# A hybrid attention block on one core: the order of all steps and the engine choices written out as lists, and small sums, casts and prefixes rewritten

## Chip, core and metric

The kernel runs on one NeuronCore of a Trainium2 chip. The metric is the device time of one execution in microseconds. Five engines work side by side, each through its own queue in program order: PE (TensorE, matmuls; PEld is its weight load), DVE (VectorE), ACT (ScalarE), POOL (GpSimd) and SP (SyncE, which here issues the DMAs). They wait for each other by semaphores only.

## What is computed

One block over 512 tokens of width 1024, all in float32, cut to the core:

```python
h = _rmsnorm(x, norm_g)
p_fox, p_ssm, p_nsa, p_mem = _split(h @ w_in, [...])
mem_kv = _rmsnorm(mem, mem_norm_g) @ w_mem_kv
o = concatenate([fox(p_fox), ssd(p_ssm), nsa(p_nsa), mem(p_mem, mem_kv)])
x = x + o @ w_out
return _rmsnorm(x, final_norm_g)
```

- fox: causal attention, 8 heads of 64, with a cumulative sum over the log of a forget gate added to the scores.
- ssd: a short convolution, then a chunked state space model (4 chunks of 128), and a norm over groups.
- nsa: for each block of 128 queries three softmaxes (over compressed blocks, selected blocks, a window), each with its own sigmoid gate, and their sum. With 512 tokens all eight blocks are selected.
- mem: attention of 4 heads of 128 over 256 memory tokens.

Each result is multiplied by silu of a gate; the four are projected by `w_out`.

## The kernel before

**Precision and tiles.** A float32 matrix is split into a rounded part and the remainder (`hi`, `lo`), and a product is three matmuls (`three`). The weights come in 75 tiles of 128 x 1024, one DMA each (`raw`), are rounded on ACT (`wh`), and the remainder is taken on POOL or DVE (`wl`, in `split`). A projection tile of 128 columns (`tile_a`) is 24 matmuls of 512 columns into one PSUM bank (`pj`), and a sink then reads the bank and makes the operands of a mixer. The output projection (`out_proj`, and `out_last` for the last mixer) writes `po` and adds it to `acc`. In the trace names without their numbers stand for tiles: `pS`, `pW` scores, `pN`, `pF`, `pM` softmax rows of nsa, fox and mem, `rs` the reciprocals of their sums, `pcp` nsa's compressed rows and `pT` their transposes, `fl`, `far`, `pt` the other rows on their way through a transpose in DRAM, `pO` the mixers' output, `pd` the prefix sums of the forget gates, `prm` the broadcast of the memory norm.

**The order.** The source runs once, in Python, and emits instructions. Everything goes through `Engine`, whose calls are noted in `Clock`, a model of all engines' times, buffers and DMAs. The projections stand in `ORDER` as background work (`Sched.todo`): one step emits three matmuls. The mixers are pipelines (`Pipe`) of stages: prep (p), ssm (s), fox (f), cmp (c), nsa (n), mem (m). In nsa, stage 0 is scores and softmax, stage 1 transposes, 2 and 3 the way to DRAM and back, 4 the product with the values and 5 the gate. `Sched.run` chooses a stage whose inputs are due by the modelled PE time, or else fills with a background step. Where an operation could run on two engines (`evac`, `rows_by`, `tt`), the engine that the model has free is taken. Buffers come from shared pools (`g` with 58 of 2 KB a partition, `b4` with 12, eight PSUM banks).

**What the change touches.** `smalls` makes gates, time steps and the forget gates' logs; `fox_bias` makes their cumulative sums: four prefix matmuls with a triangle `U`, and for blocks 1 to 3 a matmul with `ones` that adds all earlier blocks (`before`). `prep_mem` broadcasts the memory norm over all partitions by two matmuls into `prm`. In nsa's stage 0 the reciprocal of a softmax sum is made by three operations on DVE: a maximum with 1e-30, a reciprocal, a product with the gate. At the end `finish` squares a piece of a row block of the result, multiplies it by the norm's weights, and `end` makes the root and scales.

Of the kernel before, what the change touches and what calls it, by code (L numbers as in the profile page):

```python
# [32 lines left out]
LAST = 3  # L33
# [7 lines left out]
NARROW, AFTER, SLACK = 0, 500, 1000  # L41
PRE = 750

# [16 lines left out]
)  # L60
KEYS_A = [k for k in ORDER if k[0] not in ("bv", "bc", "mv") and k[0][:2] != "wo"]


class Clock:
# [4 lines left out]
    def __init__(self):  # L69
        self.t = dict.fromkeys(("PE", "ACT", "DVE", "POOL", "SP"), 700.0)  # L70
        self.dma = 0.0
        self.used = {}
        self.born = {}
        self.port = []
        self.tiled = False
        self.last = self.landed = self.sure = 0.0
        self.lanes = [0.0] * 8
        self.banks = []

# [11 lines left out]
    @staticmethod  # L91
    def box(x):

        if str(x.space).endswith("DRAM"):
# [11 lines left out]
    def at(self, x, eng=None, reading=True):  # L106
        t, u = self.born.get(x.name, 0.0), self.used.get(x.name)
        if u:
            a, b, c, d = self.box(x)
            bank = reading and str(x.space).endswith("PSUM")  # L110
            for ((e, f, g, h), by, wrote), end in u.items():
                end += self.HOP + (self.SPARE if eng == "PE" and by != "DMA" else 0)
                if by != eng and end > t and (
                        (wrote or not reading) and e < b and a < f and g < d and c < h or bank and not wrote):
                    t = end
# [5 lines left out]
    def slot(self, start, took):  # L121
# [7 lines left out]
        self.port.append((start, start + took))  # L129
        return start  # L130

    def note(self, eng, op, a, k):
# [5 lines left out]
        for x in ins:  # L138
            start = max(start, self.at(x, eng))
        for x in outs:  # L140
            if not str(x.space).endswith("DRAM"):
                start = max(start, self.at(x, eng, False))
# [3 lines left out]
        if eng == "PE":  # L146
# [8 lines left out]
            if start > self.t[eng] + 1700:  # L155
                took += 3300
        elif op == "dma_start":
            took = 430
            start = max(start, self.lanes.pop(0))
        elif eng == "ACT":  # L160
            near = str(wide[0].space).endswith("SB") if wide else True
# [8 lines left out]
        else:  # L170
            near = [x for x in wide if str(x.space).endswith("SB")]
# [8 lines left out]
            port = fast or len(near) > 1 and all(x.ap[-1][0] == 1 for x in (out, *ins))  # L180
            if any(self.box(x)[0] != self.box(out)[0] for x in wide):
# [8 lines left out]
        if op == "dma_start":  # L190
# [4 lines left out]
            both = str(out.space).endswith("DRAM") and str(ins[0].space).endswith("DRAM")  # L195
            away = str(out.space).endswith("DRAM")
# [8 lines left out]
        for xs, wrote in ((ins, False), (outs, True)):  # L205
            for x in xs:
                u = self.used.setdefault(x.name, {})
                b = self.box(x)
# [41 lines left out]

class Engine:
    def __init__(self, real, name, clock):
        self.real, self.name, self.clock = real, name, clock

    def __getattr__(self, op):
        f = getattr(self.real, op)

        def call(*a, **k):
            self.clock.note(self.name, op, a, k)
            return f(*a, **k)  # L260
# [3 lines left out]
class Sched:  # L264
    def __init__(self, clock, ready, ahead, soon, room):
        self.clock, self.ready, self.ahead, self.soon, self.room = clock, ready, ahead, soon, room
        self.todo, self.pipes = [], []
        self.done = set()

# [23 lines left out]
    def step(self):  # L293
        item = self.todo[0]
        for key, *_ in self.todo[:3]:
# [21 lines left out]

    def run(self, pipes):
        self.pipes = pipes = list(pipes)
        while pipes:  # L320
# [3 lines left out]
            now, best = self.now, None  # L324
            active = pipes[:ACTIVE]
            for pipe in active:
# [9 lines left out]
            if best[0] > now:  # L336
                t = self.due()
                if t <= now or t <= best[0]:
                    if t == math.inf:
                        raise RuntimeError(f"nothing can run: {self.todo[0][0]}, {[p.at for p in pipes]}")  # L340
                    self.fill()
# [3 lines left out]
            best[1].run(self, best[2])  # L345


class Pipe:
# [3 lines left out]
    def __init__(self, steps, stages, depth, banks, takes, keep, pre=None):  # L352
# [25 lines left out]
    def run(self, bg, k):  # L378
        i = self.at[k]
        bg.clock.last = 0.0  # L380
# [9 lines left out]
def block_kernel(ctx, tc, I, out):  # L390
    nc = tc.nc
    clock = Clock()
    V, A, P, T, Q = (Engine(e, n, clock) for e, n in (
# [3 lines left out]
    ps = ctx.enter_context(tc.tile_pool(name="ps", bufs=8, space=bass.MemoryType.PSUM))  # L397
# [3 lines left out]
    gs, bs = Store(NG), Store(NB)  # L401

    def G(name, dt=FT, w=512, p=128):
        gs.take()
        return sb.tile([p, w], dt, name=name, tag="g", bufs=NG)

    def B4(name, shape, dt=FT):
        bs.take()
        return sb.tile(shape, dt, name=name, tag="b4", bufs=NB)
# [4 lines left out]
    def SM(name, w):  # L414
        return sb.tile([128, w], FT, name=name, tag="sm", bufs=11)

    def MD(name, w):
        return sb.tile([128, w], FT, name=name, tag="md", bufs=7)

    def PS(name):  # L420
        t = ps.tile([128, 512], FT, name=name, tag="ps", bufs=8)
# [123 lines left out]

    def tt(bias, out, in0, in1, op):
# [4 lines left out]
        (V if onv + bias < onp else P).tensor_tensor(out=out, in0=in0, in1=in1, op=op)  # L551
# [134 lines left out]
    def ready(key):  # L686
        g, b = TAKES[key[0]]
        if key[0] in ("mv", "mk") and not mh:
            g, b = g + 4, b + 2
# [23 lines left out]
    def soon(key):  # L713
        if key[0] in ("mv", "mk") and (len(mh) or bg.room(4 + bg.kept(), 2)):
# [66 lines left out]
    def split_k(p, col, scale):  # L781
# [3 lines left out]
        for a in range(2):  # L785
# [3 lines left out]
            V.tensor_scalar(out=col(kx[0][a][y]), in0=p(x), scalar1=scale, scalar2=None, op0=OP.mult)  # L789
# [5 lines left out]
    def s_fq(p, key):  # L795
# [3 lines left out]
        for a in range(2):  # L799
# [3 lines left out]
            A.activation(M[a][y], ind[y, h:h + 1].to_broadcast([64, 512]), AF.Copy)  # L803
        R[key] = (R[key], M)

    def s_fk(p, key):
        l2 = B4("Rl", [128, 1024], FR)
        Rs, lo = [G("Rk", FR) for _ in range(2)], [l2[:, 512 * a:512 * a + 512] for a in range(2)]
        for a in range(2):
            x, y = slice(64 * a, 64 * a + 64), slice(64 - 64 * a, 128 - 64 * a)  # L810
            A.activation(Rs[a][x], p[x], AF.Copy)
            V.tensor_copy(out=lo[a][y], in_=cr()[y].bitcast(FT))
        for a in range(2):
            x, y = slice(64 * a, 64 * a + 64), slice(64 - 64 * a, 128 - 64 * a)
            V.tensor_copy(out=Rs[a][y], in_=p[x])
# [11 lines left out]
    def split_o(mixer):  # L827
        for j in range(4):
            if (mixer, j) in o_f and (mixer, j) not in o_hl:
                hi, lo = G("oh", FR), G("ol", FR)  # L830
                A.copy(out=hi, in_=o_f[mixer, j])
                tt(SOON, out=lo, in0=o_f[mixer, j], in1=hi.bitcast(FT), op=OP.subtract)
# [12 lines left out]
    def finish(t, i, c0, w, last):  # L845
# [15 lines left out]
        if t == 3:  # L861
            c_ = slice(384 * i, min(384 * i + 384, D))
            (V if i == 2 else P).tensor_tensor(out=fin["o"][:, c_], in0=a[:, c_], in1=g[:, c_], op=OP.mult)
        elif i == 0:
            P.tensor_tensor(out=a[:, cs], in0=a[:, cs], in1=g[:, cs], op=OP.mult)
        if last:
            fin["end"] = t, i, fs

    def end():
# [4 lines left out]
        v, r = SM("fw", 1), SM("fr", 1)  # L874
        V.tensor_reduce(out=v, in_=fs[:, 0:i + 2], axis=mybir.AxisListType.X, op=OP.add)
        P.tensor_tensor(out=r, in0=v, in1=nhalf[:, :1], op=OP.pow)
        if t == 3:
            o = fin["o"]
# [4 lines left out]
            return  # L883
        V.scalar_tensor_tensor(out=a[:, 512:1024], in0=a[:, 512:1024], scalar=r, in1=g[:, 512:1024],
# [40 lines left out]
    def out_last(t):  # L925
# [26 lines left out]
        "wo1": lambda k: out_last(k[1]) if LAST == 1 else out_proj(1, k[1]),  # L952
# [8 lines left out]
    crs, before = [], []  # L961

    def smalls():
# [20 lines left out]
        s4 = s4f.rearrange("p (t c) -> p t c", t=4)  # L984
        before.append(s4[:, 0, :])
        for t in (1, 2):
            before.append(MD("pre", 128))
            V.tensor_tensor(out=before[t], in0=before[t - 1], in1=s4[:, t, :], op=OP.add)
# [5 lines left out]
        V.tensor_scalar(out=gat, in0=gat, scalar1=1.0, scalar2=0.5, op0=OP.add, op1=OP.mult)  # L994

# [5 lines left out]
    def fox_bias():  # L1001
        s4 = s4f.rearrange("p (t c) -> p t c", t=4)
        p = PS("pd")
        for t in range(4):
# [16 lines left out]

    def evac(out_, in_):
        if clock.t["ACT"] < clock.t["DVE"]:
# [4 lines left out]
    def rows_by(x, r):  # L1028
        if clock.t["ACT"] + 100 < clock.t["DVE"]:
# [3 lines left out]

    def transposes(blocks):
        made = []
        for i in range(0, len(blocks), 4):
            n = min(4, len(blocks) - i)
            p = PS("pT")
            for k in range(n):
                T.transpose(p[:, k * 128:(k + 1) * 128], blocks[i + k], ident)  # L1040
            pt = G("pt", FT, n * 128)
            evac(pt, p[:, :n * 128])
# [877 lines left out]
```

## Time and profile before

| | |
|---|---|
| runs, median (lowest to highest) | 515.18 us (514.86 to 515.6), 3 runs |
| the profiled execution, its time | 514.93 us |
| its span, first to last instruction | 513.1 us |
| PE, DVE, ACT, POOL busy | 502.7, 356.0, 301.1, 235.2 us |
| granted TensorE clock, mean | 0.997 |
| DMA | 90.42 MB, mean 176 GB/s |

All of the kernel's instructions go through one helper line, so groups are told apart by tile names, not by lines. A row of a timeline has the start in us, the length, engine, operation, out<-in with shapes, and in brackets the engine's idle time just before it and what ended that. Matmuls are drawn with their whole length; the next one starts before the end.

### The profile page before, as it was taken

What the parts mean: (1) busy time and instruction counts of PE and PEld (TensorE: products, weight loads), DVE (VectorE), ACT (ScalarE), POOL (GpSimd) and SP (SyncE); (2) the same over time, 40 slices, a digit from 0 to 9 for tenths busy, and PEclk for the clock granted to TensorE, in tenths of its full rate; (3) what the DMA queues carried; (4) which work ended last, traced back from release to release, by engine and by line L of the source; (5) the groups of instructions that cost most, each with busy time, mean ns of one, the idle gap of its engine ahead of it and who ended that gap; (6) DMA issues with size and microseconds to landing.
All of it is one profiled execution on the core that took longest, in us unless ns stands there. A gap on an engine that the chain in (4) does not pass through costs nothing.

```text
span 513.1 us, 9049 instructions
## 1 busy us (share of the span) xinstructions
PE 502.7 (98%) x2983; PEld 420.9 (82%) x2983; DVE 356.0 (69%) x959; ACT 301.1 (59%) x679; POOL 235.2 (46%) x153
## 2 busy tenths in 40 slices
PE   8999999999999999999999999999999999999994
PEld 5898878888888888878888888788788888888884
DVE  4486774688666767788755787787778777576534
ACT  5855463594667656553456577566576666665332
POOL 3694445153244326686686332532333235224733
PEclk9999999999999999999999999999999999999998
DMA  8792234456457778342146667867877867801313
GB/s 300 310 323 95 82 124 153 138 137 197 113 166 221 222 215 283 154 168 80 42 138 222 205 171 194 271 180 223 227 220 210 244 196 211 261 25 42 123 41 123
DMA packets 70830, 90.42 MB, mean 176 GB/s; under 512 B 26352, under 2 KB 50032, under 8 KB 70784
## 3 DMA queue, kind: packets, MB, share of 16 engines
q1 hardware_dynamic: 70352, 89.27, 55.9%
q10 hardware_dynamic: 432, 0.59, 0.3%
q8 instruction: 23, 0.38, 0.3%
q14 instruction: 23, 0.19, 0.1%
HBM read 71.46 MB, written 20.53 MB: 179 GB/s over the span
## 4 chain that ended last, share of the span: by engine, by line
PE 66%; DVE 16%; ACT 7%; DMA 5%; issue 3%; SPq 2%; POOL 0%; DVEq 0%; ACTq 0%; POOLq 0%
PE pj L260 33%; PE po L260 12%; PE pb L260 6%; ACT pN L260 4%; PE pO L260 4%; DVE rs L260 4%; DVE pN L260 4%; DMA far<-fl 3%; DVE fl L260 3%; PE pS L260 3%; PE pmv L260 2%; SPq L260 2%; DVE acc L260 2%; PE pY L260 1%; DMA pt<-far 1%
## 5 line engine op out<-in xcount | busy, mean ns | idle before, releaser
L260 POOL TENSOR_TENSOR wl<-raw,wh 128x1024 fp32r<-128x1024 f32 (+1 forms) x72 | 172.0, 2396 | 222.7 <-ACT wh L260 211.4
L260 PE MATMUL pj<-hh,wh 128*128 128x512 f32 x352 | 140.8, 400 | 0.0
L260 PE MATMUL pj<-hh,wl 128*128 128x512 f32 x352 | 137.4, 390 | 0.0
L260 PE MATMUL pj<-hl,wh 128*128 128x512 f32 x352 | 137.4, 390 | 0.0
L260 ACT ACTIVATE wh<-raw 128x1024 fp32r<-128x1024 f32 (+1 forms) x72 | 74.3, 1034 | 7.5 <-DMA raw<-in_wst 6.8
L260 PEld LDWEIGHTS pj<-hh,wl 128*128 128x128 f32 x352 | 66.1, 188 | 14.4
L260 PEld LDWEIGHTS pj<-hh,wh 128*128 128x128 f32 x352 | 66.2, 188 | 13.3 <-issue 1.2
L260 PEld LDWEIGHTS pj<-hl,wh 128*128 128x128 f32 x352 | 66.2, 188 | 11.6
L260 ACT ACTIVATE pN<-pN,nm 128x128 f32<-128x128 f32 (+7 forms) x96 | 45.5, 475 | 23.2 <-DVE nm L260 21.8
L260 PE MATMUL po<-wh,oh 128*128 128x512 f32 x96 | 38.7, 404 | 0.0
L260 ACT ACTIVATE pN<-pN,rs 128x128 f32<-128x128 f32 (+3 forms) x32 | 18.1, 564 | 33.9 <-DVE rs L260 33.9
L260 PE MATMUL po<-wh,ol 128*128 128x512 f32 x96 | 37.6, 391 | 0.0
L260 PE MATMUL po<-wl,oh 128*128 128x512 f32 x96 | 37.5, 390 | 0.0
L260 DVE TENSOR_SCALAR rs<-sm 128x3 f32<-128x3 f32 x32 | 16.8, 524 | 27.9 <-ACT pN L260 27.9
L260 DVE TENSOR_TENSOR acc<-acc,po 128x512 f32<-128x512 f32 (+1 forms) x33 | 20.9, 662 | 11.8 <-PE po L260 11.8
L260 DVE STREAM_TRANSPOSE fl<-pN 128x128 f32<-128x128 f32 (+3 forms) x64 | 28.4, 485 | 0.0
L260 ACT ACTIVATE pF<-pF,nm 128x128 f32<-128x128 f32 (+3 forms) x32 | 17.7, 555 | 17.6 <-DVE nm L260 16.1
L260 DVE SCALAR_TENSOR_TENSOR xs<-x,cwh,xs 128x512 f32<-128x512 f32 x24 | 20.8, 866 | 8.1 <-ACT xs L260 7.4
L260 DVE CUSTOM_DVE_ANT_0 pN<-pS,bt 128x128 f32<-128x128 f32 (+5 forms) x80 | 21.9, 316 | 1.8 <-PE pmv L260 1.8
L260 PEld LDWEIGHTS po<-wh,ol 128*128 128x128 f32 x96 | 18.0, 188 | 4.0
L260 PEld LDWEIGHTS po<-wh,oh 128*128 128x128 f32 x96 | 18.1, 188 | 3.3 <-issue 0.3
L260 DVE RECIPROCAL rs<-sm 128x2 f32<-128x2 f32 x24 | 4.0, 166 | 23.9 <-ACT pF L260 15.2
(280 smaller groups left out, 1037.6 us busy)
## 6 DMA issues: line engine op xcount, KB each, us to landing
raw<-in_wst SPq DMA_DIRECT2D x73, 512.0 KB, 4.0
far<-fl SPq DMA_DIRECT2D x144, 64.0 KB, 2.4
pt<-far SPq DMA_DIRECT2D x36, 256.0 KB, 3.8
far<-fl SPq DMA_DIRECT2D x96, 48.0 KB, 2.0
pt<-far SPq DMA_DIRECT2D x24, 192.0 KB, 3.9
rows<-rv SPq DMA_DIRECT2D x4, 656.0 KB, 7.6
bt<-rows SPq DMA_DIRECT2D x4, 528.0 KB, 4.9
xn<-in_xn SPq DMA_DIRECT2D x4, 512.0 KB, 7.2
```

What stands on the lines that cost most here:

```text
L260: return f(*a, **k)
```

## The change

**Order.** `ORDER` is another permutation of the same weight tiles. A string `PLAN` lists every step of the main part: a letter and a digit stand for the next item of a pipeline's stage, a dot and a digit for so many background steps. If it is there, `Sched.run` follows it and decides nothing. The rules for its absence change as well (`HOLD`, stages with 64-column matmuls preferred together); they don't run.

**Engines.** `PICKS` holds, for each tile name, the engine of each use in turn (A, V for DVE, P for POOL). Of 72 subtractions for `wl`, 53 are on POOL and 19 on DVE. `evac` and `rows_by` ask it too, and copies in `s_fk` and `split_k` now go through such a choice.

**Buffers.** The program is gone through once beforehand without emitting (`lifetimes`), to know each tile's last use. Each pool's buffers become separate slots, and a new tile takes the free slot whose last use ends first by the model (`Slots`).

**Small parts.** In `fox_bias` the earlier blocks' sums are taken from the last column of each prefix and added on DVE and ACT; the tiles `before` and three matmuls go. The memory norm is stored to DRAM and read back broadcast; two matmuls go. The gates' inverse is made once, and nsa's reciprocal needs two operations. In `finish` all products with the norm's weights for the last row block are on DVE, the root ahead of the last. The SSM preparation has two stages in place of one with a wait inside. A way of mem's rows through DRAM is added for the first `MF` heads; `MF` is 0. `Clock` is changed in some constants (a matmul that follows another shape, which operations share a port).

```diff
+    def follow(self, plan):
+        pipes = {p.sign: p for p in self.pipes}
+        for c, k in zip(plan[::2], plan[1::2]):
+            self.ahead()
+            if c == ".":
+                for _ in range(int(k)):
+                    self.ahead()
+                    self.step()
+            else:
+                pipes[c].run(self, int(k))
...
+PLAN = (
...
+    "s4.8s3.9.9.1n0s4.6n0n1.5n0.1n2.5n1.2n0n3.4n1n2.1n3n0.1n4.2n1n2n3.3n5n2.1n1.2n0n0.5n1.2n4n2n4n5.7n3n5"
+    "n2n1.1n2n3.1n3n0.4n0n4n5n0.2n0.2n1.7n2.1n1n3.1n2.5n4n5.3n4n0n1.3n4n5n1n3.1n2.1n0n1n2.3n5.5n3n2.2n1n0"
+    ".1n2.1n4.2n1n4n3n0n3n4n5.1n3n4n5n5.2n0.1n5.1n1.1n3.5n2.1n4n1.1n0.1n2.1n4n5n1.1n0.5n0n3.2n2.3n1n5n2.3"
...
+PICKS = {
...
+    "wl": "PVPPPPPPPPVPVPVVVVVPPPPVPPPPVVPPVVVPPPPPVPVPPPPPPPPPPPVVPPPVPPPPPPPPPPPP",
...
     def fox_bias():
...
         for t in range(4):
-            T.matmul(p[:, t * 128:(t + 1) * 128], s4[:, t, :], U, start=True, stop=t == 0)
-            if t:
-                T.matmul(p[:, t * 128:(t + 1) * 128], before[t - 1], ones, start=False, stop=True)
+            T.matmul(p[:, blk[t]], s4[:, t, :], U, start=True, stop=True)
         gs.drop()
         c = G("cr", FR)
-        A.activation(c, p, AF.Copy, scale=-1.0)
+        sums = SM("sums", 4)
+        V.memset(sums[:, 0:1], 0.0)
+        for t in range(3):
+            V.tensor_tensor(out=sums[:, t + 1:t + 2], in0=p[:, 128 * t + 127:128 * t + 128], in1=sums[:, t:t + 1], op=OP.add)
+        for t in range(4):
+            A.activation(c[:, blk[t]], p[:, blk[t]], AF.Identity, scale=1.0, bias=sums[:, t:t + 1])
         for r in (slice(32, 64), slice(96, 128)):
-            V.scalar_tensor_tensor(out=c[r], in0=p[r], scalar=-1.0, in1=c[r].bitcast(FT),
-                                   op0=OP.mult, op1=OP.subtract)
+            for t in range(4):
+                V.scalar_tensor_tensor(out=c[r, blk[t]], in0=p[r, blk[t]], scalar=sums[r, t:t + 1],
+                                       in1=c[r, blk[t]].bitcast(FT), op0=OP.add, op1=OP.subtract)
...
     def smalls():
...
         V.tensor_scalar(out=gat, in0=gat, scalar1=1.0, scalar2=0.5, op0=OP.add, op1=OP.mult)
+        V.tensor_scalar(out=gat, in0=gat, scalar1=1e-30, scalar2=None, op0=OP.max)
+        V.reciprocal(gat, gat)
...
     def nsa():
...
-            V.tensor_scalar(out=rs, in0=sm_, scalar1=1e-30, scalar2=None, op0=OP.max)
+            gc = a * 4 + j
+            V.scalar_tensor_tensor(out=rs, in0=sm_, scalar=1e-30, in1=gat[:, b, gc:gc + 17:8], op0=OP.max, op1=OP.mult)
             V.reciprocal(rs, rs)
-            gc = a * 4 + j
-            V.tensor_tensor(out=rs, in0=rs, in1=gat[:, b, gc:gc + 17:8], op=OP.mult)
...
     def finish(t, i, c0, w, last):
...
         if t == 3:
-            c_ = slice(384 * i, min(384 * i + 384, D))
-            (V if i == 2 else P).tensor_tensor(out=fin["o"][:, c_], in0=a[:, c_], in1=g[:, c_], op=OP.mult)
+            for c_ in (slice(0, 384),) if i == 1 else (slice(384, 768), slice(768, D)) if i == 2 else ():
+                if c_.stop == D:
+                    fin["r"] = root(fs, i)
+                V.tensor_tensor(out=fin["o"][:, c_], in0=a[:, c_], in1=g[:, c_], op=OP.mult)
...
     def mem_r():
...
+        r = rsq(ms, 2, 1.0 / D, "rm")
+        Q.dma_start(out=rmd.rearrange("t p -> p t"), in_=r)
...
     def prep_mem():
-        pr = PS("prm")
-        bcast_rows(pr, r, 2)
+        pr = G("prm", FT, 256)
+        Q.dma_start(out=pr, in_=bass.AP(tensor=rmd.tensor, offset=rmd.offset, ap=[[0, 128], [1, 256]]))
+        yield
```

More of the change, by code (lines that the diff above doesn't have):

```diff
@@ L156, in note @@
                 took += 3300
+            wide = n >= 500 and not exact
+            if wide and not self.wide:
+                took += 40
+            self.wide = wide
         elif op == "dma_start":
@@ L179, in note @@
                 lag = 140
-            port = fast or len(near) > 1 and all(x.ap[-1][0] == 1 for x in (out, *ins))
-            if any(self.box(x)[0] != self.box(out)[0] for x in wide):
+            port = fast or len(near) > 1 and n >= 64
+            if any(b[0] != boxes[1][0][0] for x, b in zip(ins, boxes[0]) if self.size(x) > 1):
                 took, lag = took + 90, 12
@@ L324, in run @@
             now, best = self.now, None
+            if self.began is not None and now < self.began + HOLD and self.due() <= now:
+                self.fill()
+                continue
             active = pipes[:ACTIVE]
+            same = [(p, k) for p in active for k in p.tiled if p.due(self, k) <= now] if self.clock.tiled else []
+            if same:
+                same[0][0].run(self, same[0][1])
+                self.began = None
+                continue
             for pipe in active:
@@ L345, in run, with __init__ @@
             best[1].run(self, best[2])
+            self.began = None
 class Pipe:
-    def __init__(self, steps, stages, depth, banks, takes, keep, pre=None):
+    def __init__(self, steps, stages, depth, banks, takes, keep, pre=None, tiled=()):
+        self.tiled = tiled
         self.steps, self.stages, self.depth, self.banks, self.takes = steps, stages, depth, banks, takes
@@ L379, in run @@
         i = self.at[k]
+        assert k == 0 or i < self.at[k - 1]
+        assert k not in self.pre or all(key in bg.done for key in self.pre[k](self.steps[i])[0])
+        bg.trace.append(self.sign + str(k))
         bg.clock.last = 0.0
@@ L867, in finish, with root @@
             fin["end"] = t, i, fs
+    def root(fs, i):
+        v, r = SM("fw", 1), SM("fr", 1)
+        V.tensor_reduce(out=v, in_=fs[:, 0:i + 2], axis=mybir.AxisListType.X, op=OP.add)
+        P.tensor_tensor(out=r, in0=v, in1=nhalf[:, :1], op=OP.pow)
+        return r
     def end():
@@ L1020, in softmax_neg, with free @@
         return t
+    def free():
+        return "A" if clock.t["ACT"] < clock.t["DVE"] else "V"
     def evac(out_, in_):
-        if clock.t["ACT"] < clock.t["DVE"]:
+        if pick(out_, free()) == "A":
             A.copy(out=out_, in_=in_)
@@ L1028, in rows_by @@
     def rows_by(x, r):
-        if clock.t["ACT"] + 100 < clock.t["DVE"]:
+        t, n = max(clock.at(x, "-"), clock.at(r, "-")), clock.size(x)
+        onv = clock.slot(max(t, clock.t["DVE"]), 130 + 0.52 * n, False) + 130 + 0.52 * n
+        if pick(x, "A" if max(t, clock.t["ACT"]) + 110 + 0.83 * n < onv + EVEN else "V") == "A":
             A.activation(x, x, AF.Copy, scale=r)
@@ L1032, in rows_by, with flip @@
             V.tensor_scalar(out=x, in0=x, scalar1=r, scalar2=None, op0=OP.mult)
[L1034 to L1042, printed above, removed]
[L1043 to L1045 removed]
     def flips(w):
         return 1 if 2 * w <= 512 else 2
[L1051 to L1053 removed]
+    def flip(tiles, w, held=2):
+        b, per = w // 128, min(len(tiles), 512 // w)
         made = []
[L1055 to L1057 removed]
+        for c in range(0, len(tiles), per):
             t = G("fl", FT, per * w)
@@ L1469, in ssm_pre, with ssm_rows @@
         V.tensor_copy(out=dA2[:, 32:64], in_=dA)
-        bg.until(clock.ready([dA2]))
+        pre.extend((nacs, dte, decR))
+        return dA2
+    def ssm_rows(dA2):
         pa = PS("pa")
         T.matmul(pa[:64, :128], dA2, U, start=True, stop=True)
-        ar = sb.tile([64, 128], FR, name="ar", tag="md", bufs=7)
+        ar = MD("ar", 128, FR)[:64]
         A.copy(out=ar, in_=pa[:64, :128])
@@ L1724, in s2 @@
             t = st[s]
+            if s[0] < MF:
+                st[s] = flip([t[:, i * 256:(i + 1) * 256] for i in range(2)], 256, 1)
+                return
             p = PS("pT")
@@ L1804, in block_kernel @@
         bg.add(key, adders[key[0]](key))
-    bg.until(clock.ready([s4f, *before]))
+    bg.until(clock.ready([s4f]))
     cr()
     made = {"fox": fox, "cmp": compress, "mem": mem, "nsa": nsa, "ssm": ssm, "pre": prep}
-    bg.run([made[n]() for n in PIPES])
+    pipes = []
+    for n in PIPES:
+        pipes.append(made[n]())
+        pipes[-1].sign = n[0]
+    bg.run(pipes)
+    lives.trace, lives.picked = bg.trace, picked
     while bg.todo:
@@ L1900, in _layout, with lifetimes, build @@
     }
-def build(nc, arrays):
+def lifetimes(arrays):
+    import concourse.bacc as bacc
+    lives = Lives()
+    try:
+        build(bacc.Bacc("TRN2", target_bir_lowering=False, num_devices=1, dynamic_dma_scratch_size=1024), arrays, lives)
+    except Rehearsed:
+        pass
+    return [lives.last.get(name, 0) for name in lives.made]
+def build(nc, arrays, lives=None):
+    lives = lives or Lives(lifetimes(arrays))
     I = {n: nc.dram_tensor("in_" + n, v.shape, mybir.dt.from_np(v.dtype), kind="ExternalInput").ap()
```

299 lines of the change are left out of this document (203 added, 96 removed), and 18 rows, old and new, of the table ORDER.

## The prediction

> **What bounds the kernel now.** I read the page first, then the busy time by stretches, PE's list of waits, the groups by form, and the timeline around PE's longest wait and around the end.
>
> ```profile
> span 513.1 us, 9049 instructions
> ...
> PE 502.7 (98%) x2983; PEld 420.9 (82%) x2983; DVE 356.0 (69%) x959; ACT 301.1 (59%) x679; POOL 235.2 (46%) x153
> ...
> PEclk9999999999999999999999999999999999999998
> ```
>
> ```profile
> 41.00:130.00 89.00, 89.00 (x417) 73.86 (x417) 64.33 (x138) 50.33 (x95) 36.86 (x17) 1.00 0.44 138
> ...
> 270.00:442.00 172.00, 170.34 (x1078) 142.73 (x1077) 128.65 (x489) 111.69 (x306) 64.50 (x43) 1.00 0.73 212
> ...
> 485.00:513.00 28.00, 21.45 (x106) 18.04 (x105) 10.75 (x23) 9.03 (x23) 9.02 (x9) 0.94 0.20 75
> ```
>
> ```profile
> PE pT L260 <- DVE pcp L260: 1.5, 4, 0.7
> ...
> PE pb L260 <- ACT uh L260: 0.4, 1, 0.4
> PE pb L260 <- DVE wh L260: 0.2, 1, 0.2
> ```
>
> PE is busy for 502.7 of 513.1 us at the full clock; the columns of a stretch are PE, PEld, DVE, ACT, POOL. Between 41 and 130 us PE has no hole, DVE works 64 of 89 us. Between 270 and 442 us, the NSA mixer's stretch, 1.7 us are open. PE's own list has four waits after the start, 1.5 us together, all of the small transpose pT for the tile pcp. The last stretch has 6.5 us without PE: the end of the program. So a reordering has three things to win: matmuls that are no longer issued, the four waits, and the end. What the other engines gain or lose elsewhere costs nothing until PE waits for it.
>
> **Matmuls removed.** Two edits take work from PE: the prefix sums of the forget gates no longer come from matmuls with `before` (pd), and the row broadcast of the memory norm (prm) goes through DRAM.
>
> ```profile
> 50.07 1.56 PE pd L260 x14
> ```
>
> ```profile
> L260 PE MATMUL pd<-ones,pre 128*128 128x128 f32 x4 | 0.8, 275 | 0.0
> ...
> L260 PE MATMUL prm<-cst,rmr 128*128 128x128 f32 x4 | 0.6, 274 | 0.0
> ...
> L260 PE MATMUL pd<-ones,s 128*128 128x128 f32 x2 | 0.4, 275 | 0.0
> ```
>
> Each of the five matmuls stands in the trace as two records. Fourteen pd records take 1.56 us, 0.111 each; the mean of 275 ns is an instruction's whole length and overlaps the next. Ten records go: **-1.1 us**, all on PE, so all on the path. The ends are close: 0.9 if one is shadowed by a neighbour, 1.4 if the return to 512-column matmuls after prm costs as much as one or two records more. No other matmul is added or dropped: the list holds every stage of every mixer once, and the stages with 64-column matmuls stand in it in as many separate runs as in the trace's order, so PE changes its shape as often as before. The list as such saves no PE time; it can only take waits away.
>
> **The four waits.** This is the longest, in the timeline of three engines:
>
> ```profile
> 324.24 0.39 PE L260 MATMUL po<-wl,oh 128*128 128x512 f32 x1
> 324.47 0.40 PE L260 MATMUL po<-wh,ol 128*128 128x512 f32 x1
> 325.56 0.28 PE L260 MATMUL pT<-cst,pcp 128*96 128x128 f32 x1 [0.69 <-DVE pcp L260]
> ```
>
> ```profile
> 319.82 4.77 POOL L260 TENSOR_TENSOR wl<-raw,wh 128x1024 fp32r<-128x1024 f32 x2 [9.05 <-ACT wh L260]
> ```
>
> ```profile
> 323.35 1.39 DVE L260 TENSOR_SCALAR rs<-sm 128x3 f32<-128x3 f32 x1 [0.81 <-ACT pN L260]
> ...
> 324.98 0.16 DVE L260 TENSOR_TENSOR rs<-rs,gat 128x3 f32<-128x3 f32 x1
> 325.18 0.23 DVE L260 TENSOR_SCALAR pcp<-pN,rs 128x8 f32<-128x8 f32 x1
> ```
>
> Matmuls follow each other every 0.23 us and are drawn 0.39 long, so a wait costs PE 0.16 more than the idle time shown: four waits of 1.5 us in sum cost 1.5 + 4 x 0.16 = 2.1 us. Here a 3-element TENSOR_SCALAR on DVE took 1.39 us and ended with POOL's weight subtraction (324.59 against 324.74).
>
> ```profile
> L260 DVE TENSOR_SCALAR rs<-sm x32: 168/169/1619, 272.9 to 429.1; 128x3 f32<-128x3 f32 x32
> ...
> L260 DVE TENSOR_TENSOR rs<-rs,gat x32: 161/163/169, 273.3 to 429.6; 128x3 f32<-128x3 f32 x32
> ...
> L260 DVE TENSOR_SCALAR pcp<-pN,rs x32: 229/236/244, 273.6 to 429.8; 128x8 f32<-128x8 f32 x8, 128x16 f32<-128x16 f32 x8, 128x24 f32<-128x24 f32 x8, 128x32 f32<-128x32 f32 x8
> ```
>
> Undisturbed it takes 169 ns. The edit folds this operation and the product with the gate into one SCALAR_TENSOR_TENSOR; the gate's inverse is made once at the start. One operation of three goes, 0.20 us by the starts above, in each of 32 steps: 6.4 us of DVE, and pcp is 0.2 us earlier. Whether the long wait goes too the trace can't say: the third and fourth operations never waited, but they always came behind one that already had. It may simply move to pcp, the next TENSOR_SCALAR. The list decides more: it sets how much PE work lies between a softmax (n0) and its transposes (n1). With every dot as one background step (three matmuls of 0.23 in eight steps of nine, 0.61 us), most distances are 6 to 16 us. I take two thirds of the 2.1: **-1.4 us**, between 0 (the waits only move) and -2.1 (all gone). Two thirds, since the shorter chain and the POOL work taken away both act on the same late tile.
>
> The Trainium skill, page SBUF — State Buffer, section Who interferes with whom, says that an operation of DVE with two inputs in SBUF also waits for a POOL instruction that reads SBUF, for that one's whole length. By that rule the new operation, which reads sums and gates, would wait as the old one did, and the first case would turn into the first rival. The trace agrees that POOL's end releases the TENSOR_SCALAR; for the new form no run yet shows it.
>
> **The end.**
>
> ```profile
> 505.04 1.49 DVE L260 SCALAR_TENSOR_TENSOR acc<-acc,fr,fgn 128x512 f32<-128x512 f32 x1 [0.65 <-POOL fr L260]
> 506.45 0.74 DVE L260 TENSOR_TENSOR acc<-acc,po 128x256 f32<-128x256 f32 x2
> 507.23 0.99 DVE L260 TENSOR_TENSOR og<-acc,fgn 128x256 f32<-128x256 f32 x1
> 508.14 0.14 DVE L260 TENSOR_REDUCE fw<-fs 128x1 f32<-128x4 f32 x1
> ```
>
> ```profile
> 506.94 1.00 POOL L260 TENSOR_TENSOR og<-acc,fgn 128x384 f32<-128x384 f32 x1 [0.96 <-DVE acc L260]
> 508.36 0.54 POOL L260 TENSOR_TENSOR fr<-fw,nhalf 128x1 f32<-128x1 f32 x1 [0.42 <-DVE fw L260]
> ```
>
> ```profile
> 507.62 0.19 ACT L260 ACTIVATION_READ_ACCUMULATOR sq<-acc 128x1 f32 x1
> ```
>
> The last sum of squares is there at 507.81, yet the reduction fw starts at 508.14, behind a 256-element product that took 0.99 us beside POOL's. The edit gives all these products to DVE and puts the reduction ahead of the last one, which then runs beside POOL's power. Without POOL's product the 1.49 us operation is shorter too and the two additions start with PE's end; half of the first comes off the sum of squares. I put fw at 507.6 to 507.7: **-0.5 us**, between -0.2 (only the order helps) and -0.9 (the additions no longer wait at all).
>
> **What lies beside other work.** The list of choices moves 18 whole weight subtractions and a half from POOL to DVE; the other picks change hands about evenly.
>
> ```profile
> L260 DVE TENSOR_TENSOR ol<-of,oh 128x512 fp32r<-128x512 f32 x4 | 2.5, 684 | 0.0
> ...
> L260 DVE SCALAR_TENSOR_TENSOR yc<-xs,hd,pY 128x128 f32<-128x128 f32 x16 | 4.5, 341 | 0.0
> ```
>
> At twice 0.684, 1.4 us each, eight of them fall into 41 to 130 us: 11 us beside 25 of idle DVE. The eight smaller operations and three sums for cr add about 8 x 0.34 + 3 x 0.16 less the old two, under 2 us, tens of microseconds before the first product with cr. Both cost 0; if that cover were gone, a sink would come late and PE stand for what is missing, at most one operation of 1.4 us at a time.
>
> The memory norm's rows now cross DRAM, and their store stands on SP's queue until POOL has the root:
>
> ```profile
> 50.01 0.71 POOL L260 TENSOR_TENSOR rmr<-rmv,nhalf 128x2 f32<-128x2 f32 x1 [6.65 <-DVE x L260]
> ```
>
> ```profile
> 43.39 30.55 SPq L260 DMA_DIRECT2D raw<-in_wst  x6
> ```
>
> ```profile
> 61.42 1.04 ACT L260 ACTIVATE wh<-raw 128x1024 fp32r<-128x1024 f32 x1
> ```
>
> The weight load that was issued at 43.39 stands behind it until about 51, with the root at most half a microsecond later than before (two operations on the gates stand ahead of it on DVE, two sums no longer do). Its tile is first read at 61.42, so ten microseconds remain for a landing. 0, and some of its slack is spent. Choosing a buffer by its modelled end, the split of the SSM preparation into two stages and the new order of tiles are costed at 0 for the same reason: no wait of PE after the start is for a bank, a buffer or a load, so only a new one could count. The memory mixer's path through DRAM and the holding rule are switched off by their zeros.
>
> **Sum.** -1.1 - 1.4 - 0.5 = -3.0 us. The profiled execution took 514.93 us for its span of 513.1, which would become 511.9; the median of the runs is 0.25 above it, so I predict 515.18 - 3.0 = **512.2 us**.
>
> **Rivals.** First, the waits only move: pcp waits for POOL in place of rs. For it speaks that 1.39 us ended with POOL's instruction; against it, the greater distances and less POOL work. -1.6 us, 513.6.
>
> Second, slower: a late pcp. PE runs in order, and in six places the list leaves little between n0 and n1: about 4.1, 4.3, 4.7, 5.1, 5.3 and 5.9 us, 29.4 in sum (the 4.3, of pair 1 and block 1: five dots, 3.1 us, and two sets of score matmuls, an estimated 1.2). The trace has both short and long ways from the first matmul to pcp:
>
> ```profile
> 367.97 0.40 PE L260 MATMUL pS<-kh,L 128*128 128x288 f32 x1
> ...
> 412.36 0.35 PE L260 MATMUL pS<-kh,L 128*128 128x416 f32 x1
> ```
>
> ```profile
> 371.00 0.23 DVE L260 TENSOR_SCALAR pcp<-pN,rs 128x16 f32<-128x16 f32 x1
> ...
> 419.23 0.24 DVE L260 TENSOR_SCALAR pcp<-pN,rs 128x24 f32<-128x24 f32 x1
> ```
>
> 3.3 and 7.1 us. At 6 us in all six places PE would stand 36 - 29.4 = 6.6 us; with today's waits gone that is 6.6 - 2.1 - 1.6 = +2.9, 518.1. It decides by more than 0.2% from a mean of 5.7 us on. Against it: the long ways came where DVE had other work queued, and that order is rewritten too.
>
> Third, nothing net: shorter stalls of that kind, 3.0 in sum in place of 2.1, with half the end's gain lost, or a lost DMA or weight load of the same size. About 515.
>
> **How the numbers follow.** 0.2% is 1.03 us, about what a measurement here can tell from no change. Chances: forecast 0.62, waits move 0.20, slower 0.10, nothing net 0.08. The forecast's own range is 510.4 (all terms at their far ends, -4.4, and part of the 0.6 us of waits in the first projection) to 513.8. The range for 8 in 10 takes in the first rival with 1 us for its ends: 510.4 to 514.6. Faster: 0.61 + 0.18 = 0.79; same 0.11; slower 0.10.
>
> **What would show it.** Right: pd with 8 records and no prm; PE's waits for pcp under 1 us; fw starting 0.4 to 0.6 us sooner after PE's last matmul; PE's busy time down by 1. Wrong: pT waiting in the six places for pcp, pcp taking over a microsecond beside wl, DVE near its full time between 41 and 130 us with PE waiting for a sink, or a wait for raw near 66 us.

## The result and the profile after

The changed kernel takes **518.59 us** (median of 4, 518.09 to 518.84) where the kernel before takes 515.02: a ratio of 1.0068 (1.0050 to 1.0085). The forecast was 512.2 with 510.4 to 514.6 around it, so it was wrong in sign. The profiled execution took 518.76 us for a span of 517.0.

The page of the changed kernel, its opening rows:

```profile
span 517.0 us, 9000 instructions
...
PE 507.0 (98%) x2973; PEld 420.3 (81%) x2973; DVE 359.0 (69%) x965; ACT 302.0 (58%) x680; POOL 186.4 (36%) x127
```

PE has ten records less (2983 to 2973) and yet is busy 4.3 us longer, 507.0 against 502.7. POOL has lost 49 us of work, as the list of choices says. PE's list of waits doesn't explain it; its first rows:

```profile
PE pw L357 <- DVE warm L357: 1.3, 1, 1.3
PE pT L357 <- DVE pcp L357: 0.8, 1, 0.8
PE pn L357 <- DVE sq L357: 0.5, 1, 0.5
PE pb L357 <- DVE fv L357: 0.3, 1, 0.3
```

After the start it holds 2.1 us in five waits, before 2.1 in six. The four waits of pT are one. Three of the four signs that the prediction named for "right" are there: pd with 8 records and no prm, waits for pcp under 1 us, and fw sooner behind PE's last matmul. The fourth, PE's busy time down by 1 us, is not: it is up by 4.3. In PE's timeline of the changed kernel pd has 8 records and 1.05 us; in the tail fw starts 1.41 us after PE's last matmul, before it was 1.97 (506.17 to 508.14):

```profile
50.09 1.05 PE L357 MATMUL pd<-cst,s 128*128 128x128 f32 x8
...
510.35 0.28 PE L357 MATMUL po<-lh,ol 128*128 128x256 f32 x1
...
511.76 0.16 DVE L357 TENSOR_REDUCE fw<-fs 128x1 f32<-128x4 f32 x1 [0.17 <-ACT sq L357]
```

The loss is in the matmuls themselves. This is the longest stretch of uninterrupted pj matmuls, its first and last row in PE's timeline: before, 104 matmuls; after, 102.

```profile
69.13 0.39 PE L260 MATMUL pj<-hl,wh 128*128 128x512 f32 x1
...
92.50 0.39 PE L260 MATMUL pj<-hh,wl 128*128 128x512 f32 x1
```

```profile
67.54 0.39 PE L357 MATMUL pj<-hh,wh 128*128 128x512 f32 x1
...
91.10 0.40 PE L357 MATMUL pj<-hh,wl 128*128 128x512 f32 x1
```

Start to start that is 23.37 / 103 = 226.9 ns before and 23.56 / 101 = 233.3 ns after, with the same shapes, the same types and, in both stretches, the full clock. Over all pj matmuls that follow each other without a hole (starts under 260 ns apart) the mean is 228.2 before and 233.0 after; 1,056 of them at 4.8 ns more are about 5 us. The time by stretches hid it: a stretch in which PE never stands reads as 100% busy at any pace.

```profile
69.20:92.40 23.20, 23.20 (x104) 19.20 (x103) 4.82 (x7) 3.55 (x6) 1.00 0.49 153
```

```profile
67.60:90.80 23.20, 23.20 (x101) 18.70 (x100) 5.08 (x8) 4.69 (x8) 1.00 0.30 94
```

The counts in brackets tell: in the same 23.2 us PE touched 104 matmuls before and 101 after.

### The profile page after: what moved, and what is told of

It is laid out like the page before. It is cut to its first block, busy times and chain, and to the rows that moved or that the text cites. A ratio compares the mean times of both kernels' runs of the same rounds, so it can differ in the third digit from the quotient of the medians.

```text
span 517.0 us, 9000 instructions
## 1 busy us (share of the span) xinstructions
PE 507.0 (98%) x2973; PEld 420.3 (81%) x2973; DVE 359.0 (69%) x965; ACT 302.0 (58%) x680; POOL 186.4 (36%) x127
## 4 chain that ended last, share of the span: by engine, by line
PE 88%; DVE 4%; ACT 2%; issue 2%; DMA 2%; POOLq 0%; POOL 0%; DVEq 0%; ACTq 0%
PE pj L357 47%; PE po L357 16%; PE pO L357 7%; PE pS L357 5%; PE pb L357 5%; PE pmv L357 2%; PE pW L357 1%; DMA xt<-in_xT 1%; PE pT L357 1%; PE pY L357 1%; DVE pN L357 1%; DMA raw<-in_wst 1%; PE pcm L357 1%; DVE yc L357 1%; ACT pN L357 1%
## 5 line engine op out<-in xcount | busy, mean ns | idle before, releaser
L357 POOL TENSOR_TENSOR wl<-raw,wh 128x1024 fp32r<-128x1024 f32 (+1 forms) x53 | 127.6, 2412 | 248.4 <-ACT wh L357 213.7
L357 PE MATMUL pj<-hh,wl 128*128 128x512 f32 x352 | 139.3, 396 | 0.0
L357 PE MATMUL pj<-hl,wh 128*128 128x512 f32 x352 | 139.1, 395 | 0.0
L357 DVE TENSOR_TENSOR wl<-raw,wh 128x1024 fp32r<-128x1024 f32 (+1 forms) x20 | 23.3, 1167 | 5.8 <-ACT wh L357 5.3
L357 DVE SCALAR_TENSOR_TENSOR rs<-sm,gat 128x3 f32<-128x3 f32 x32 | 6.6, 207 | 27.9 <-ACT pN L357 27.9
L357 ACT ACTIVATE pN<-pN,rs 128x512 f32<-128x512 f32 (+3 forms) x28 | 15.9, 594 | 11.4 <-DVE rs L357 11.4
L357 DVE SCALAR_TENSOR_TENSOR xs<-x,cwh,xs 128x512 f32<-128x512 f32 x24 | 18.0, 751 | 5.8 <-ACT xs L357 5.1
```

## The experiments

Two explanations stood at first. One: the new order puts other engines' reads and writes beside the matmuls, and these slow PE. The other: the change gives each buffer a tag of its own (`g0` to `g57`, `sm0` and so on in place of one pool), tiles are laid out in the order of their first use, and so the operands have other addresses. No trace holds addresses; by those of the built program before, the operands of pj, pb and po lie so that the starts of the moving and the stationary operand differ by a multiple of 256 bytes. After, in pj they differ by 224 modulo 256, because the 16-byte tile `rx` and the small slots, rounded to 32 bytes, stand between hh and wh; in po they differ by several values.

### Layout alone: a_pad, b_w0, b_g0w0, b_g0

a_pad is the changed kernel with one tile widened; the order on every engine is unchanged.

```diff
-    rx = C1("rx", [128, 4])
+    rx = C1("rx", [128, 16])[:, 0:4]
```

> The changed kernel with the tile rx 48 bytes longer and nothing else: all instructions and their order are the same; every tile allocated after rx starts 32 bytes later, so that the moving operands hh and hl start 32 bytes past a multiple of 64, as in the kernel before, and no longer at a multiple of 64. Theory A (where the operands start sets PE's pace): the 512-column matmuls go from about 233 back to about 228 ns, some 1500 of them, so 518.6 falls by 5 to 7 us to 511.5 to 513.5. Theory B (the new order or the moved engine work slows PE): nothing changes, 518 to 519, pace 233.

The three others are the kernel before, again in an unchanged order: in b_w0 the weight tiles are moved by 32 bytes, in b_g0w0 these and the operands in G tiles by 32 each, in b_g0 the G tiles by 32 and the weights by 64:

```diff
-    nhalf = C1("nhalf", [128, 8])     # b_w0, b_g0
+    nhalf = C1("nhalf", [128, 16])
-    x0 = C1("x0", [128, 632])         # b_g0w0, b_g0
+    x0 = C1("x0", [128, 640])
```

> The kernel before with nhalf 32 bytes longer: the weight tiles wh and wl start at a multiple of 64, all other matmul operands stay 32 past one; the order is the same. Theory A, if it is the moving operand's start that counts: the projections pj (moving hh, hl) keep 227 ns, the output projections po (moving wh, wl) go to about 233, 372 of them: 515 + 2 = 517. Theory A, if a difference between the two operands counts: pj and po both slow, 515 + 6 = 521. Theory B: 515.

> The kernel before with x0 32 bytes longer: all matmul operands start at a multiple of 64; the order is the same. Theory A, if the moving operand's start counts: pj and po at 232 to 233 ns, 520 to 521. If a difference between the operands counts: 227 ns, 515. Theory B: 515.

> The kernel before with x0 and nhalf both 32 bytes longer: hh and hl start at a multiple of 64, wh and wl 32 past one, as in the changed kernel; the order is the same. Theory A in either form: pj slows to about 233 ns, 519 to 521. If only the moving operand counts, po stays at 227 and the time is 519. Theory B: 515.

Measured, with the pace of pj over the long stretch and the distance of its operands modulo 256:

| kernel | distance in pj | pace of pj, ns | time, us | ratio to before (95%) |
|---|---|---|---|---|
| before | 0 | 226.9 | 514.61 | 1 |
| b_g0w0 | 0 (both moved) | 226.9 | 514.70 | 1.0000 (0.9991 to 1.0009) |
| b_w0 | 224 | 233.3 | 519.08 | 1.0088 (1.0072 to 1.0103) |
| b_g0 | 224 | 233.3 | 519.33 | 1.0091 (1.0077 to 1.0105) |
| after | 224 | 233.3 | 518.59 | 1.0068 (1.0050 to 1.0085) |
| a_pad | 0 | 226.9 | 515.03 | 1.0012 (1.0001 to 1.0022) |

Eight more floats in a constant cost the kernel before 4.5 us; twelve more in `rx` give the changed kernel about 3 back (3.6 between the two times, 2.9 by the ratios, since before was 515.02 beside the one and 514.61 beside the other). It isn't the place of one operand (b_g0w0 moves both and loses nothing), it is the distance between the two. The size came out smaller than expected: 521 for b_w0, 519 to 521 for b_g0. That the order slows PE is refuted for this part: b_w0 has the order of before and the pace of after.

By its expectation a_pad should have been at about 512, and wasn't. Two things remained in its profile: po still ran at 231.3 ns, and PE's list had a new wait, the first below.

```profile
PE pcm L357 <- DMA w<-in_w: 1.8, 1, 1.8
...
PE pj L357 <- DVE wl L357: 0.5, 1, 0.5
```

### Which distance: c_256, b_s128, b_s64

In a_pad the operands of po are 0, 64, 128 or 192 apart, by the slot that each tile got. c_256 pads five constants and tiles of the changed kernel, so that all of pj, pb, po and pmv are at 0:

```diff
-    rx = C1("rx", [128, 4])
+    rx = C1("rx", [128, 16])[:, 0:4]
-    nv = C1("nv", [128, 4, 296])
+    nv = C1("nv", [128, 4, 304])[:, :, 0:296]
...
-        kx.extend([B4(f"k{x}{a}", [128, 1056], FR) ...
+        kx.extend([B4(f"k{x}{a}", [128, 1088 if x == "l" and lives.known else 1056], FR) ...
-    cbh = C1("cbh", [128, 8])
+    cbh = C1("cbh", [128, 24])[:, 0:8]
```

(and 32 columns more for `decR`). b_s128 and b_s64 are the kernel before with 128 or 64 bytes more in `nhalf`.

> The changed kernel with its tiles padded so that the two operands of every 512-column matmul of pj, pb, pmv and po start a multiple of 256 bytes apart; the order on every engine is that of the changed kernel (two memsets of kl are 32 columns longer). In a_pad the distance was 0 in pj, but 0, 64, 128 and 192 in po, and po stayed at 231.4 ns while pj fell to 228.3. Theory A (the pace follows the distance, and only a distance that stays 0 modulo 256 gives the short pace): po falls to about 228.5, 356 matmuls x 3 ns = 1.05 us less than a_pad, so about 514.0 where the kernel before has 514.6. Theory B (the distance matters modulo 64 alone, and po is slow in the new order for another reason): po stays at 231, time as a_pad, 515.0.

> The kernel before with one pad of 128 bytes: the operands of pj, pb and most of po, which start a multiple of 256 bytes apart, are now 128 modulo 256 apart. Nothing else differs. Theory A (only 0 modulo 256 gives the short pace): pj above 230 ns, 516 to 519 us. Theory B (modulo 64 alone): pj 228.3, 514.6.

> The same with 64 bytes: operands 64 or 192 modulo 256 apart. Theory A: pj above 230 ns, 516 to 519 us. Theory B: pj 228.3, 514.6.

c_256: 514.44 us, ratio 0.9997 (0.9988 to 1.0005); po, from start to start where no hole lies between, is at 228.0 ns, in a_pad 231.3 and before 228.4. b_s128: 518.54, 1.0078 (1.0065 to 1.0092), pj at 232.4 ns. b_s64: 518.58, 1.0080 (1.0064 to 1.0095), pj, there 192 apart, at 233.3. So 128, 192 and 224 cost pj 5.5 to 6.4 ns a matmul, and of the distances tried only 0 modulo 256 had the short pace. The size of the loss isn't the same everywhere: po, 64 apart in b_s64, is at 231.0, and 32 apart in b_w0 at 233.3. The first and last of the 104 matmuls of the long stretch in b_s128:

```profile
70.14 0.39 PE L260 MATMUL pj<-hl,wh 128*128 128x512 f32 x1
...
94.08 0.40 PE L260 MATMUL pj<-hh,wl 128*128 128x512 f32 x1
```

### The late w1: c_256h

With the pace repaired, c_256 was only level with before. The first wait of a_pad's list, 1.8 us, is also in c_256, 1.0 us in its profile. SyncE's queue tells why. First a_pad, then c_256h, which exchanges one weight load with the four loads of w1 and nothing else:

```profile
195.18 1.89 SPq L357 DMA_DIRECT2D pt<-far  x4
197.21 5.46 SPq L357 DMA_DIRECT2D raw<-in_wst  x2
202.71 1.94 SPq L357 DMA_DIRECT2D w<-in_w  x4
```

```profile
197.36 0.36 SPq L358 DMA_DIRECT2D raw<-in_wst  x1
197.76 2.30 SPq L358 DMA_DIRECT2D w<-in_w  x4
202.49 0.33 SPq L358 DMA_DIRECT2D raw<-in_wst  x1
```

The second weight load has no free buffer until 202.5, and w1 stood behind it; pcm wants w1 at about 210.5. Before, w1 was issued at 197.88.

```diff
+            if not wait and clock.hold:      # in load(): no early weight load
+                return
...
+            self.clock.hold = w1 - 2 * HELD <= 2 * n <= w1   # four steps up to c0
```

> c_256 with one edit on SP's queue alone: the weight load (raw) that stood ahead of the four loads of w1 stands behind them. In the trace of a_pad this raw load holds SP until 202.7, w1 is issued at 202.7 to 204.6 against 197.9 to 199.6 before, and PE waits 1.8 us for w. Theory A (the late w1 costs PE up to 1.8 us): the wait pcm for w is gone, w1 is issued at about 198, and the time is 1 to 1.8 us under c_256 in the runs that had the wait; about 513.0. Theory B (only the name of the wait changes): PE waits for raw, wh or wl instead, and the time is that of c_256.

512.57 us, ratio 0.9964 (0.9951 to 0.9976): 1.9 us under c_256, and pcm no longer waits. The new order of the DMA queue had cost that much. At the long pace it can't be seen: in the changed kernel's list of PE's waits pcm doesn't stand.

### The parts of the sum, undone one by one: u_mm, u_rs, u_end

All three on c_256h.

```diff
+        for t in (0, 1, 2, 3, 3):            # u_mm, after the four pd matmuls
+            T.matmul(p[:, blk[t]], s4[:, t, :], U, start=True, stop=True)
```

> c_256h (512.57 where before has 514.59, a difference of -2.0 us) with five 128-column f32 matmuls more, each a repeat of one of the four pd matmuls at the same place, as many as the change took away. The output is the same. Prediction's step (ten records of 0.111 us on the path): +1.1, that is 0.9 us under before. Rival (the removed matmuls stood where PE would have waited anyway): under +0.3.

512.95 us, ratio 0.9963 (0.9950 to 0.9977), from c_256h no difference that the intervals resolve; by the medians it is 0.4, neither the +1.1 nor the under +0.3 of the expectation. The timelines of PE, c_256h first:

```profile
49.35 1.05 PE L358 MATMUL pd<-cst,s 128*128 128x128 f32 x8
50.24 0.31 PE L358 MATMUL pa<-dA,cst 128*128 128x32 f32 x2
...
66.98 0.49 PE L358 MATMUL pj<-hh,wl 128*128 128x512 f32 x1 [0.52 <-DVE wl L358]
```

```profile
49.18 2.17 PE L358 MATMUL pd<-cst,s 128*128 128x128 f32 x18
51.18 0.31 PE L358 MATMUL pa<-dA,cst 128*128 128x32 f32 x2
...
67.15 0.50 PE L358 MATMUL pj<-hh,wl 128*128 128x512 f32 x1
```

From pd to pa it is 0.89 and 2.00: the five matmuls cost 1.11, as predicted. But the lead of 0.94 at pa is 0.17 at 67 us, because c_256h stands 0.52 there for wl: most of what was saved was waited away. The prediction's "all on PE, so all on the path" holds only as long as no later wait absorbs it.

```diff
-            V.scalar_tensor_tensor(out=rs, in0=sm_, scalar=1e-30, in1=gat[...], op0=OP.max, op1=OP.mult)
-            V.reciprocal(rs, rs)
+            V.tensor_scalar(out=rs, in0=sm_, scalar1=1e-30, scalar2=None, op0=OP.max)
+            V.reciprocal(rs, rs)
+            V.tensor_tensor(out=rs, in0=rs, in1=gat[...], op=OP.mult)
```

> c_256h with the old three operations for rs (maximum, reciprocal, product with the gate) and the gate not inverted. Theory A (the shorter chain matters): PE's waits for pcp grow from 0.9 to between 1.5 and 2.5 us, rs's maximum is seen again with over 1 us beside POOL's wl, and the time rises by 0.5 to 1.5 us. Theory B (the list alone took the long waits away): waits for pcp as in c_256h within 0.3 us and the time within 0.4 us. The Trainium skill, SBUF - State Buffer, section Who interferes with whom, would have the new operation with two SBUF inputs wait as long as the old one; by it u_rs and c_256h show rs of the same largest length.

521.24 us, ratio 1.0125 (1.0111 to 1.0138): 8.7 us over c_256h, far beyond the expectation. (The planner's clock moves two weight loads by one or two places on SP too; nothing else differs.) PE's waits:

```profile
PE pT L358 <- DVE pcp L358: 3.6, 2, 2.5
PE pW L358 <- DVE ct L358: 1.4, 1, 1.4
```

The largest is at 289.75. DVE's row and POOL's row ahead of it:

```profile
283.82 2.76 DVE L358 TENSOR_SCALAR pN<-pN,rs 128x256 f32<-128x256 f32 x2
```

```profile
283.98 2.44 POOL L358 TENSOR_TENSOR wl<-raw,wh 128x1024 fp32r<-128x1024 f32 x1 [1.78 <-ACT wh L358]
```

In c_256h the same two operations take 0.61 us, and the second begins ahead of POOL's subtraction. Delayed by 0.2 us, it begins behind the subtraction's start and ends just after it (286.58, POOL 286.42); the next pcp and PE are late. It was the second time: at the first step of nsa the same had happened.

```profile
272.28 2.65 DVE L358 TENSOR_SCALAR pN<-pN,rs 128x128 f32<-128x128 f32 x2
```

```profile
272.45 2.39 POOL L358 TENSOR_TENSOR wl<-raw,wh 128x1024 fp32r<-128x1024 f32 x1 [1.06 <-ACT wh L358]
```

So 8.7 us is not the price of 32 small operations but of where they push their neighbours in this one list; that each step is as tight isn't shown. Nor does the old form by itself wait longer: all 32 operations from sm to rs took 16.8 us before, 7.0 in u_rs with the old form and 6.7 in c_256h with the new one. By these sums it was the list, which moves work off POOL, that took the time away, and not the folding.

```diff
+            c_ = slice(384 * i, min(384 * i + 384, D))     # u_end: as before
+            (V if i == 2 else P).tensor_tensor(out=fin["o"][:, c_], ...)
...
+            o, r = fin["o"], root(fs, i)                   # fw behind the last product
```

> c_256h with the end as before: the products og of 384 columns on POOL, the reduction fw behind the last product on DVE. Prediction's step: fw starts 0.5 us later after PE's last matmul and the time rises by 0.5 (0.2 to 0.9). Rival, from the tail of the traces (6.93 us from PE's last start to the end before, 6.64 in a_pad): +0.3.

513.49 us, ratio 0.9976 (0.9966 to 0.9985). PE's last matmul and DVE's last fw:

```profile
504.46 0.28 PE L358 MATMUL po<-lh,ol 128*128 128x256 f32 x1
...
506.43 0.14 DVE L358 TENSOR_REDUCE fw<-fs 128x1 f32<-128x4 f32 x1
```

1.97 us, exactly as before. The span ends 7.11 us after that matmul (511.57), in c_256h 6.58: undone, the end costs 0.5 us. By the medians u_end is 0.9 over c_256h, and the intervals of the two overlap.

### The lists taken away: c_free

```diff
-PLAN = ( ... )
+PLAN = ""
-PICKS = { ... }
+PICKS = {}
```

(with other pads, so that the distances of these matmuls are 0 again).

> The changed kernel with the lists PLAN and PICKS emptied, so that the scheduler with its own costs chooses each step and engine as the kernel before does, padded so that the operands of the 512-column matmuls start a multiple of 256 bytes apart. The order of the weights stays that of the change. Theory A (the lists are worth their stalls): PE's waits in sum are 2 us or more above c_256h's 3.2, and the time is 514 to 517. Theory B (the lists as such save no PE time, as the prediction says of PE's work, and waits are small either way): within 1 us of c_256h, 512.0 to 513.5.

538.73 us, ratio 1.0467 (1.0452 to 1.0481), 26 us over c_256h and far outside both theories. PE's waits are 19.8 us in 15 groups; the first two, and the row of the granted clock:

```profile
PE pT L325 <- DVE pcp L325: 3.3, 2, 2.0
PE pn L325 <- DVE sq L325: 3.1, 2, 2.1
```

```profile
PEclk9999999999999999769899989999999999999998
```

The waits are 16.6 us more than c_256h's 3.2. The other 9.5 us are PE's busy time, 510.6 us in place of 501.1: the granted clock, 0.978 in the mean in place of 0.998, fell to 0.77 between 215 and 245 us, where PE was busy 22.9 of 30 us. That the waits brought the clock down isn't shown.

So the lists carry this source. What they are worth against the scheduler of before isn't shown by it, since the new order of the weights stays and was chosen together with them.

### The standing of SP, and both layouts side by side: c_best, a_sp

The wait for wl at 67 us led back to SP: its weight load is issued at 52.56, behind the store of the memory norm's root. c_best is c_256h with one weight load ahead of that store; a_sp is the changed kernel, with its own layout, and the same two edits on SP's queue.

```diff
+        load(state["load"] + (state["load"] < state["split"] + RAW))
         Q.dma_start(out=rmd.rearrange("t p -> p t"), in_=r)
```

> c_256h with two neighbours on SP's queue exchanged: one weight load (raw) goes ahead of the store of the memory norm's root (rmd), which waits for POOL. Nothing else differs. Theory A (the standing of SP, costed at 0, is what makes wl late at 67 us): the load is issued at about 43 in place of 52.6, PE's wait of 0.5 us for wl is gone, and the time is 0.5 to 0.7 us under c_256h's 512.57: 511.9, or 2.6 under before. Theory B (wl is late for another reason, DVE or ACT): the wait stays and the time with it.

> The same two edits on SP's queue (w1 ahead of one weight load, one weight load ahead of rmd) in the changed kernel as it is, with its own layout. Theory A (with the slow pace these waits were covered; the layout alone carries the loss): 518.6 as the changed kernel, pj above 230 ns. Theory B (they cost something there too): 517 to 518.

c_best takes **512.10 us**, ratio 0.9953 (0.9941 to 0.9966), 0.5 under c_256h, which the intervals alone don't resolve; a_sp 518.14, ratio 1.0067 (1.0053 to 1.0081). SP in c_256h, then in c_best:

```profile
52.06 0.39 SPq L358 DMA_DIRECT2D rmd<-rmr  x1
52.56 5.81 SPq L358 DMA_DIRECT2D raw<-in_wst  x3
```

```profile
43.37 0.33 SPq L358 DMA_DIRECT2D raw<-in_wst  x1
51.95 0.39 SPq L358 DMA_DIRECT2D rmd<-rmr  x1
```

PE's waits in c_best; then the matmul that stood for wl, PE's last one and the fw behind it:

```profile
PE pw L358 <- DVE warm L358: 1.3, 1, 1.3
PE pT L358 <- DVE pcp L358: 0.9, 1, 0.9
PE pn L358 <- DVE sq L358: 0.5, 1, 0.5
```

```profile
66.31 0.50 PE L358 MATMUL pj<-hh,wl 128*128 128x512 f32 x1
...
503.67 0.28 PE L358 MATMUL po<-lh,ol 128*128 128x256 f32 x1
...
505.05 0.16 DVE L358 TENSOR_REDUCE fw<-fs 128x1 f32<-128x4 f32 x1 [0.17 <-ACT sq L358]
```

c_best and a_sp issue the same instructions in the same order on every engine; they differ in pads. Their 6.0 us are the layout's. And a_sp is not distinguishable from the changed kernel (ratios 1.0067 and 1.0068): at the slow pace no gain of the two edits on SP's queue can be told.

## Why the prediction was wrong, step by step

**The step that failed** is the sentence "Choosing a buffer by its modelled end, the split of the SSM preparation into two stages and the new order of tiles are costed at 0". Its reason, that no wait of PE is for a bank, a buffer or a load, speaks only of when a buffer is free. The same edit also decides where each buffer lies, and that set the pace of some 1,500 matmuls: +6.0 us (a_sp against c_best), more than the whole forecast gain. "No other matmul is added or dropped" was true, but it is a count and says nothing of the duration. None of the rivals named it. The slower one said 518.1, near the 518.59 that was measured, but by luck: it put the loss on late pcp, and that isn't where it came from. The third, with its lost weight load, is what c_256 shows once the pace is repaired: 514.44, level with before.

**Loads.** The same sentence missed that a reordered queue makes new waits: w1 behind a weight load, 1.9 us between c_256 and c_256h. It could have been looked for in the list before the run: the weight loads stand where the background steps ask for them, and only two such steps lie between c0 and c1.

**SP standing for the root**, "0, and some of its slack is spent": the load was issued at 52.56 (the prediction had about 51), 9 us later than before, and its slack wasn't enough: in c_256h wl came late. It costs PE 0.5 us and what a wait adds at 67 us, shown by c_best, where that wait is gone and the matmul starts at 66.31 in place of 66.98.

**What was right, and what only looks so.** Two terms held. The five matmuls cost 1.11 in u_mm (predicted 1.1). The end: in c_best fw starts 1.38 us after the last matmul in place of 1.97 (predicted 0.4 to 0.6 sooner), and undone in u_end it cost 0.5 of span (predicted 0.5); from before to c_best, though, the tail behind PE's last matmul shrank by 0.3 alone, from 6.93 to 6.6.

The waits were mis-sized. The forecast took 1.4 us out of the four waits of pT. In c_best these 1.5 us in four waits have become 0.9 in one, but a wait of 0.5 for sq is new: by the prediction's own 0.16 for each wait that is 0.1 + 2 x 0.16, 0.4 us. The two waits at the start, 0.6 us, are gone as well, and gave nothing: the first pj matmul starts at 41.74 before and at 41.96 in c_best.

```profile
41.74 0.39 PE L260 MATMUL pj<-hh,wh 128*128 128x512 f32 x1
```

```profile
41.96 0.39 PE L358 MATMUL pj<-hh,wh 128*128 128x512 f32 x1
```

PE's last matmul is 2.50 us earlier in c_best (503.67 and 506.17). With 1.1 for the matmuls and 0.4 for waits, 1.0 us is in no term of the sum, and no run undoes it. So that c_best stands at 512.10, where 512.2 was predicted, is luck in part: beside it before had 514.62, a gain of 2.5 where 3.0 was forecast, for a kernel with other pads and two DMAs at other places.

**The rivals.** That the wait moves to pcp didn't happen: pcp took at most 0.25 us. The waits of rs became fewer: 12 of 32 operations took over 0.18 us before, 4 in c_256h and 4 in the changed kernel. The late pcp of the second rival came in one place, but not in one of its six: in c_best the scores of that step start at 342.84, 8.5 us ahead of pT at 351.32, and pcp comes late behind other work of DVE. In the six close places PE didn't stand. The prediction's bound, a mean of 5.7 us, left POOL out; in u_rs it was POOL that turned 0.2 us into 2.

**The rule on inputs in SBUF.** In c_256h one of the 32 new rs operations took 1.02 us, and its end, 361.26, is that of POOL's subtraction, 361.24:

```profile
360.24 1.02 DVE L358 SCALAR_TENSOR_TENSOR rs<-sm,gat 128x3 f32<-128x3 f32 x1 [0.81 <-ACT pN L358]
```

```profile
358.84 2.40 POOL L358 TENSOR_TENSOR wl<-raw,wh 128x1024 fp32r<-128x1024 f32 x1 [2.12 <-ACT wh L358]
```

The Trainium skill, page SBUF — State Buffer, section Who interferes with whom, says that such an operation contends with a POOL instruction that reads SBUF, and that the shared ports are an exclusive lock. By these rows the trace agrees for the new form too; the old form's longest in u_rs is 1.05 us. Folding the operation didn't take the wait away; three more of the 32 took 0.23 to 0.50 us, and in the other 28 the list keeps them clear of POOL's work.

## What to carry to other kernels

An edit that renames, splits or reorders buffers moves tiles, and the place of a tile is part of a matmul's price: compare the start-to-start time of a long uninterrupted stretch of the same matmuls before looking for waits, for a busy share of 100% says nothing of pace. Print the operands' addresses of both programs and pad until their distances are those of the faster one. And when a stage grows faster, look again at each queue in its order: two DMAs whose cost couldn't be told at 233 ns a matmul cost 2.3 us at 227.

## What the runs showed of the hardware that was not expected

A 128x512 fp32r matmul started every 226.9 ns when the starts of its moving and stationary operands differed by a multiple of 256 bytes, and in pj every 232.4 to 233.3 ns when they differed by 128, 192 or 224 modulo 256; b_g0w0 shows that moving both together changes nothing. In po it was 233.3 at 32, 231.0 at 64, and 231.3 in a_pad, where the distance changed from one matmul to the next. There it isn't the matmul's own distance alone: by the built program's order, po's matmuls in a_pad at distance 0 that are followed by another at 0 took 230.7 ns in the mean, as against 228.0 in c_256, where all are at 0. Why the distance matters, no run shows; nor was it tried for other types, for shorter matmuls, or for distances under 32 bytes.
